# Moving two gate projections out of the opening of an attention, and filling its steps with the output projection

## The chip, the cores and the metric

The kernel runs on one core of a Trainium2 chip. The metric is the device time of one execution in microseconds (us). The kernel before takes 2390.4 us (median of three runs, 2390.4 to 2392.38).

## The reference

A two-layer encoder trunk on 1024 frames of width 1024, all in fp32. Only the mixer of the first layer matters here:

```python
def even_mixer(h, w_in, ..., w_out):
    z = h @ w_in
    uv = gelu(z[..., :1024]); u, v = uv[..., :512], uv[..., 512:]
    q, k, vv, f_logit = the other columns of z      # 8 heads x 64
    y_a = u * (W_s rms_norm(v) + b_s)               # 4 groups x 128 channels
    y_b = forgetting_attention(q, k, vv, log_sigmoid(f_logit))
    return concatenate([y_a, y_b]) @ w_out          # 512 + 512 rows of w_out

def forgetting_attention(...):                      # causal, 8 heads, 8 query blocks of 128
    logits = q.k / 8 + (cumulated log f);  p = softmax(logits);  out = p @ v
```

The residual add, a cross-attention and a feed-forward block follow, and the second layer has another mixer. The change touches none of these.

## The kernel before, in words

**Number format.** Every fp32 operand is split into a high and a low half of a narrower type (fp32r). A product of two operands is three matmuls: high by high, high by low, low by high. All of them are recorded at L539 (`mm`), the low halves at L551 (`low`, on VectorE) or L549 (on GpSimd), the high halves at L557 (`split`, a cast on ScalarE) or, for weights, at L688.

**Order.** The program builds a list of tasks (`self.add`), and `run()` emits them one after the other. A scheduler then arranges the instructions of each engine by data dependence and priority; each engine runs its own list in order. So a task that stands earlier in the list makes its instructions come earlier on several engines at once.

**The gates.** u is computed in four groups of 128 channels. `gate_u(g)` issues 48 matmuls of 128x512 over h, which VectorE reads (L1151) and ScalarE's gelu (L1153) passes on; `gated(g)` is VectorE's product (L1182), which makes y_a of that group.

**The attention.** It runs as a pipeline over 32 steps, 8 heads of 4 query-block pairs (s = 0..31 in the loop). The pipeline opens two steps early (s = -2, -1) with scores alone. Each step has: two score groups on TensorE of widths 128 to 1024 (0.3 to 2 PSUM banks), VectorE's row maximum (L1423), ScalarE's exp (L1425), VectorE's reciprocal (L1429), GpSimd's normalisation (L1430), transposes on TensorE (L1440), cast and low half of the transposed weights (L1443, L551), the product with the values (L539), and a copy and an add (L1474, L1478). exp and gelu need different tables on ScalarE: a change between them is a recorded ACT_TABLE_LOAD.

**The fill.** The half of the output projection that reads y_a does not depend on the attention. It is cut into 32 units (`fill_unit`) of six 128x512 matmuls, which are handed out to the attention's steps. All units share one PSUM bank. After every second unit VectorE adds the bank onto rows of x (L1501), which SP loads from the buffer `xs` in memory (L1494, 512 KB) and stores back (L1505) two units later, one load and one store for four units. The fill needs y_a split into halves: `y_split(g)`, one group a task (L557, L551 of 128x1024).

**Memory.** The split operands live in an arena (`arena_r`). Its first 16K columns, region a, hold h as long as a gate is still to be computed. `close_h` gives them back. Splits of y_a and of the values (`values_in`, L1402) are placed with "ab": in region a where it is free, else in region b.

**The opening of before.** Gates 2 and 3 are tasks of the steps s = -2 and s = -1, behind these steps' scores; h is given back at s = -1, and one y_a group is split in each of the steps s = -2..1. The fill begins at s = 2: two units a step in s = 2..7, one in s = 8..27, none in s = 28..31.

Of the kernel before, what the change touches and what calls it, by code (L numbers as in the profile page):

```python
# [473 lines left out]
class Trunk:  # L474
# [66 lines left out]
    def add(self, fn, ws=(), boost=0):  # L541
        self.tasks.append(Task(fn, ws, boost))
# [331 lines left out]
    def even_in(self):  # L874
# [272 lines left out]
        def gate_u(g, w):  # L1147
            ps = self.B.get(2)
            self.dense(ps, self.h_parts(), self.lhs_from(w, P), KD)
            u = gu[g] = self.F.get(S, "ab")  # L1150
            nc.vector.tensor_tensor(out=u.ap, in0=ps.ap, in1=self.rbc.ap, op=ALU.mult)  # L1151
            ps.free()
            nc.scalar.activation(out=u.ap, in_=u.ap, func=AF.Gelu_apprx_tanh)  # L1153
# [27 lines left out]
        def gated(g):  # L1181
            nc.vector.tensor_tensor(out=self.u[g].ap, in0=self.u[g].ap, in1=gu[g].ap, op=ALU.mult)  # L1182
            gu.pop(g).free()

        wu = [self.w_block(w_in, 0, KD, g * P, P) for g in range(4)]
# [3 lines left out]
        self.add(lambda: (mixed(), gated(0)))  # L1189
        self.add(lambda: (self.fox_open(), gate_u(1, wu[1])), [wu[1]])  # L1190
        self.add(lambda: gated(1))
        self.gates = [[Task(lambda g=g: gate_u(g, wu[g]), [wu[g]]), Task(lambda g=g: gated(g))] for g in (2, 3)]

    def mixing_weights(self):

# [172 lines left out]
    def fox(self):  # L1368
# [39 lines left out]
        def scores(h, p, e):  # L1408
            i = 2 * p + e
            w = (i + 1) * P  # L1410
            qa, ka, qb, kb = (t.ap for t in sets[h % 2])
            ps = self.B.get(1 if w <= 512 else 2, *self.pS)
            q = slice(i * P, (i + 1) * P)
            for c0 in range(0, w, 512):
                n = min(512, w - c0)
                o = ps.ap[:, c0:c0 + n]
                diag = c0 + n == w
                self.mm(o, qa[0:68, q], ka[0:68, c0:c0 + n], True, False)
                self.mm(o, qb[:, q], kb[:, c0:c0 + n], False, not diag)
                if diag:  # L1420
                    self.mm(ps.ap[:, w - P:w], self.identr, self.maskr, False, True)
            m, rs, ri = self.tiny(1), self.tiny(1), self.tiny(1)
            nc.vector.tensor_reduce(out=m, in_=ps.ap[:, 0:w], op=ALU.max, axis=AX.X, negate=True)  # L1423
            pt = self.F.get(w, "ab")
            nc.scalar.activation(out=pt.ap, in_=ps.ap[:, 0:w], func=AF.Exp, bias=m, scale=1.0, accum_out=rs)  # L1425
            ps.free()

            def norm():
                nc.vector.reciprocal(out=ri, in_=rs)  # L1429
                nc.gpsimd.tensor_scalar(out=pt.ap, in0=pt.ap, scalar1=ri, scalar2=1.0, op0=ALU.mult, op1=ALU.mult)  # L1430
            self.defer(norm)
            st["p"][h, i] = pt

        def turn(h, p, c):
            ps = self.B.get(1, *self.pT)
            p0, p1 = st["p"][h, 2 * p], st["p"][h, 2 * p + 1]
            pieces = [(p0, 2 * c), (p1, 2 * c)] + ([(p0, 2 * c + 1)] if c < p else []) + [(p1, 2 * c + 1)]
            n = len(pieces) * P
            for s, (t, j) in enumerate(pieces):
                nc.tensor.transpose(out=ps.ap[:, s * P:(s + 1) * P], in_=t.ap[:, j * P:(j + 1) * P],  # L1440
                                    identity=self.ident)
            th, tl = self.R.get(n, "ab"), self.R.get(n, "ab")
            nc.scalar.copy(out=th.ap, in_=ps.ap[:, 0:n])  # L1443
            st["t"][h, p, c] = th, tl

            def rest():
                self.low(tl.ap, ps.ap[:, 0:n], th.f)
                ps.free()
            self.defer(rest)
            if c == p:  # L1450
                p0.free()
                p1.free()

        def mix(h, p):
            ps = self.B.get(1, *self.pM)
            pr = h // 2
            v = [t.ap.rearrange("p (b e d) -> p b e d", e=2, d=P) for t in st["v"][pr]]
            nj = 2 * p + 2
            for j in range(nj):
                th, tl = st["t"][h, p, j // 2]  # L1460
                lone = j == nj - 1
                c0 = (j % 2) * 256
                n = P if lone else 256
                o = ps.ap[:, 256 - n:256]
                for x, t in enumerate((th, tl)):
                    self.mm(o, v[j // 4][:, j % 4, h % 2, :], t.ap[:, c0:c0 + n], j == 0 and x == 0, lone and x == 1)
            for c in range(p + 1):
                for t in st["t"].pop((h, p, c)):
                    t.free()
            if h % 2 == 0 and p == 0:  # L1470
                self.yb[pr] = self.F.get(S, "b")
            lo = (h % 2) * 64
            tmp = self.F.get(256, "ab")
            nc.scalar.copy(out=tmp.ap[0:64], in_=ps.ap[64:128, 0:256])  # L1474
            yb = self.yb[pr]

            def rest():
                nc.vector.tensor_tensor(out=yb.ap[lo:lo + 64, p * 256:(p + 1) * 256],  # L1478
                                        in0=ps.ap[0:64, 0:256], in1=tmp.ap[0:64], op=ALU.add)
                ps.free()  # L1480
                tmp.free()
                if h == HEADS - 1:
                    self.part_split(3, p * 256, (p + 1) * 256)
            self.defer(rest)

        def y_split(g):
            self.y_a.append(self.split(self.u[g].ap, "ab", S))
            self.u[g].free()
# [26 lines left out]
        add = lambda fn, ws=(): self.add(fn, ws)  # L1515

        def before(h, p):
            if p == 0 and 1 <= h and h + 1 < HEADS:
                heads_in(h + 1)
            if p == 2 and h % 2 == 1 and h + 1 < HEADS:  # L1520
                values_in(h // 2 + 1)
            n = h * 4 + p
            if n == 28:
                for t in sets[0]:
                    t.free()
            if n == 30:
                for t in self.y_a:
                    t[0].free()
                    t[1].free()
                self.open_part(3)  # L1530
            if n in WHOLE:
                self.y_whole(WHOLE.index(n))
# [8 lines left out]
        def close_h():  # L1541
            for b in range(NB):
                self.free_h(b)
            self.rbc.free()
        add(begin)
        wb = [self.w_block(self.a["e_w_out"][0], 512, 4, mp * 256, 256) for mp in range(4)]
        self.wb = wb
        for s in range(-2, len(steps) + 1):
            nxt = steps[s + 2] if s + 2 < len(steps) else None
            cur = steps[s] if 0 <= s < len(steps) else None  # L1550
            old = steps[s - 1] if s >= 1 else None
            turns = [lambda cur=cur, c=c: turn(*cur, c) for c in range(cur[1] + 1)] if cur else []
            if nxt:
                add(lambda nxt=nxt: (scores(*nxt, 0), before(*nxt)))
            if s == len(steps) - 1:
                add(lambda: self.b_part(0, range(0, 3)), [wb[0]])
            if turns:
                add(turns.pop(0))
            if nxt:
                add(lambda nxt=nxt: scores(*nxt, 1))  # L1560
            for t in turns:
                add(t)
            if s == len(steps):
                add(lambda: self.b_part(1, range(0, 3)), [wb[0]])
            if old:
                def fin(old=old):
                    mix(*old)
                    h, p = old
                    if h % 2 == 1 and p == 3:
                        for t in st["v"].pop(h // 2):  # L1570
                            t.free()
                add(fin)
            if s < 0:
                self.tasks.extend(self.gates[s + 2])
            if s == -1:
                add(close_h)
            if s < 2:
                add(lambda g=s + 2: y_split(g))
                continue
            for _ in range(2 if s < 8 else 1):  # L1580
                if fill:
                    self.tasks.append(fill.pop(0))
        assert not fill
# [811 lines left out]
```

## Time and profile before

| | before |
|---|---|
| median of three runs | 2390.4 us |
| the profiled execution's own time | 2389.92 us |
| its span | 2388.1 us |
| mean granted TensorE clock | 0.994 |
| TensorE busy | 2337.4 us (98%) |
| VectorE busy | 1705.6 us (71%) |
| ScalarE busy | 1024.2 us |
| GpSimd busy | 743.0 us |

The shares are means over the whole program. The attention of the first layer lies between about 300 us (its first scores) and 500 us (its last products), and it is read from rows of that stretch. In the rows, PE is TensorE, DVE VectorE, ACT ScalarE, POOL GpSimd, and SPq the issues of SP's DMA queue. Bracketed numbers are idle time before a row's first instruction, with what ended it.

### The profile page before, as it was taken

The page shows a single profiled execution, that of the slowest core. Times are in us where ns is not written, and L with a number is a line of the kernel's source. Part 1 is how long each engine was busy: PE and PEld are TensorE (multiplying, and loading weights), DVE is VectorE, ACT ScalarE, POOL GpSimd, SP SyncE. Part 2 cuts the span into 40 slices and gives each one's busy share as a digit, 9 for nine tenths or more (in the row PEclk, how much of TensorE's full clock was granted, in tenths as well). Part 3 has the DMA queues.
Part 4 walks back from the last instruction along what each step waited for, and adds up shares of the span by engine and source line. Part 5 has one row for each costly group of instructions (what it writes and reads, how often), then busy time and mean ns, then how long its engine had stood idle before and what let it go on. Part 6 is the DMA issues. An engine that isn't in the chain of part 4 may idle for free. (4 is left out here: it accounts for less than half of the span.)

```text
span 2388.1 us, 31149 instructions
## 1 busy us (share of the span) xinstructions
PE 2337.4 (98%) x11358; PEld 1976.5 (83%) x11358; DVE 1705.6 (71%) x2505; ACT 1024.2 (43%) x1866; POOL 743.0 (31%) x745
## 2 busy tenths in 40 slices
PE   7999999999999999999999899999999999999999
PEld 7999879988888878887888788888877887877887
DVE  5456457864898888978677553356879988887666
ACT  6346356755554444445224221146544444444221
POOL 6542333343333343433011310033333334342000
PEclk9999999999999999999999999999999999999999
DMA  7336325431224444438873121021233444357783
GB/s 235 119 133 214 97 81 151 125 124 45 89 70 160 142 149 139 153 131 295 279 267 117 50 65 44 28 79 45 89 101 138 150 141 168 118 194 260 254 289 92
DMA packets 227074, 335.57 MB, mean 141 GB/s; under 512 B 12864, under 2 KB 128664, under 8 KB 226920
## 3 DMA queue, kind: packets, MB, share of 16 engines
q1 hardware_dynamic: 214544, 289.32, 37.1%
q0 software_dynamic: 12192, 44.21, 5.2%
q8 instruction: 89, 1.46, 0.3%
q14 instruction: 65, 0.53, 0.1%
q10 hardware_dynamic: 184, 0.05, 0.0%
HBM read 226.44 MB, written 107.09 MB: 140 GB/s over the span
## 5 line engine op out<-in xcount | busy, mean ns | idle before, releaser
L539 PE MATMUL psum_t<-arena_r 128*128 128x512 f32 (+4 forms) x10304 | 2255.4, 378 | 34.2 <-DVE arena_r L551 10.7
L539 PEld LDWEIGHTS psum_t<-arena_r 128*128 128x128 f32 (+1 forms) x10304 | 1856.2, 189 | 380.1 <-DVE arena_r L551 18.3
L551 DVE TENSOR_TENSOR arena_r<-arena_f,arena_r 128x512 fp32r<-128x512 f32 (+4 forms) x803 | 672.1, 857 | 167.5 <-PE psum_t L539 53.2
L256 ACT CAST arena_r<-arena_f 128x512 fp32r<-128x512 f32 (+2 forms) x504 | 282.4, 584 | 429.4 <-PE psum_t L539 252.6
L2026 POOL TENSOR_TENSOR arena_f<-arena_f 128x512 f32<-128x512 f32 x88 | 164.4, 1874 | 462.4 <-ACT arena_f L2025 462.3
L247 DVE TENSOR_TENSOR arena_f<-arena_f 128x512 f32<-128x512 f32 (+2 forms) x288 | 205.5, 717 | 81.4 <-DMA arena_f<-w_down 48.5
L1973 DVE TENSOR_TENSOR arena_f<-psum_t,arena_f 128x512 f32<-128x512 f32 x208 | 141.7, 685 | 51.6 <-PE psum_t L539 36.0
L2062 ACT CAST arena_r<-arena_f 128x512 fp32r<-128x512 f32 x140 | 86.8, 621 | 160.0 <-DVE arena_f L2033 58.2
L2058 POOL TENSOR_TENSOR arena_f<-arena_f 128x512 f32<-128x512 f32 x80 | 132.0, 1669 | 37.1 <-DVE arena_f L2033 35.6
L2004 DVE TENSOR_TENSOR arena_f<-psum_t,arena_f 128x512 f32<-128x512 f32 x160 | 106.4, 686 | 36.0 <-PE psum_t L539 35.7
L688 ACT CAST arena_r<-arena_f 128x1024 fp32r<-128x1024 f32 (+1 forms) x57 | 59.0, 1042 | 128.9 <-PE psum_t L539 90.3
L803 POOL TENSOR_TENSOR arena_f<-arena_f 128x1024 f32<-128x1024 f32 x21 | 60.6, 2884 | 127.8 <-ACT arena_f L802 61.9
L551 DVE TENSOR_TENSOR arena_r<-psum_t,arena_r 128x512 fp32r<-128x512 f32 (+3 forms) x124 | 84.6, 703 | 18.7 <-ACT arena_r L1443 6.8
L2025 ACT ACTIVATE arena_f<-arena_f 128x512 f32<-128x512 f32 x88 | 55.6, 632 | 81.6 <-DVE arena_f L2024 81.6
L236 POOL DMA_DIRECT2D arena_f<-w_down x38 | 30.3, 799 | 191.7 <-DVE arena_r L551 107.1
L1430 POOL TENSOR_SCALAR arena_f<-arena_f,small 128x640 f32<-128x640 f32 (+6 forms) x64 | 49.5, 781 | 108.8 <-DVE small L1429 104.7
L2033 DVE TENSOR_TENSOR arena_f<-arena_f 128x512 f32<-128x512 f32 x88 | 76.4, 868 | 4.5 <-POOL arena_f L2026 0.5
L2024 DVE TENSOR_TENSOR arena_f<-arena_f 128x512 f32<-128x512 f32 x88 | 66.2, 752 | 1.1 <-ACT arena_f L831 1.1
L562 POOL TENSOR_TENSOR small<-small,mhalf 128x4 f32<-128x4 f32 (+1 forms) x64 | 63.7, 995 | 5.2
L1425 ACT ACTIVATE arena_f<-psum_t,small 128x640 f32<-128x640 f32 (+6 forms) x64 | 47.5, 745 | 23.1 <-DVE small L1423 20.2
L2261 POOL TENSOR_TENSOR arena_f<-arena_f 128x1024 f32<-128x1024 f32 x4 | 10.4, 2598 | 139.5 <-DVE arena_f L2213 139.5
L1753 POOL TENSOR_SCALAR arena_f<-arena_f,small 128x256 f32<-128x256 f32 x64 | 33.3, 538 | 65.2 <-DVE small L1750 50.8
(192 smaller groups left out, 1533.9 us busy)
## 6 DMA issues: line engine op xcount, KB each, us to landing
pq<-arena_r SPq DMA_DIRECT2D x140, 512.0 KB
arena_r<-pq SPq DMA_DIRECT2D x280, 256.0 KB
arena_f<-w_gate SPq DMA_DIRECT2D x22, 1024.0 KB
arena_f<-w_up SPq DMA_DIRECT2D x22, 1024.0 KB
arena_r<-qk SPq DMA_DIRECT2D x48, 256.0 KB
qk<-arena_r POOLq DMA_DIRECT2D x16, 512.0 KB, 4.1
arena_f<-xa_wkv SPq DMA_DIRECT2D x16, 512.0 KB
arena_f<-xs SPq DMA_DIRECT2D x16, 512.0 KB
```

The source lines that it names most:

```text
L247: getattr(T.nc, self.adds).tensor_tensor(out=out, in0=a, in1=b, op=what)
L256: T.nc.scalar.copy(out=hv, in_=src)
L539: self.nc.tensor.matmul(out=out, lhsT=lhsT, rhs=rhs, start=start, stop=stop, skip_group_check=again)
L551: getattr(self.nc, eng).tensor_tensor(out=out, in0=src, in1=high, op=ALU.subtract)
L562: self.nc.gpsimd.tensor_tensor(out=out, in0=in_, in1=self.mhalf[:, 0:in_.shape[-1]], op=ALU.pow)
L1973: nc.vector.tensor_tensor(out=o, in0=bank[q].ap, in1=o if other is None else other, op=ALU.add)
L2004: nc.vector.tensor_tensor(out=o, in0=bank[q].ap, in1=o, op=ALU.add)
L2024: nc.vector.tensor_tensor(out=q, in0=q, in1=r, op=ALU.mult)
L2026: nc.gpsimd.tensor_tensor(out=q, in0=q, in1=r, op=ALU.mult)
L2033: nc.vector.tensor_tensor(out=c[j].ap[:, o], in0=c[j].ap[:, o], in1=s.ap[:, o], op=ALU.mult)
L2058: nc.gpsimd.tensor_tensor(out=out, in0=a, in1=b, op=ALU.subtract)
L2062: nc.scalar.copy(out=t.ap[:, 0:512], in_=src)
```

## The change

Gates 2 and 3 become ordinary tasks right behind gate 1, before the attention is opened. h is given back before the attention opens, so the values of the first two heads and all four y_a splits are placed where h was. Two y_a groups are split in s = -2 and two in s = -1. The fill begins at s = -1: two units a step in s = -1..5, one in s = 6..23, none in s = 24..31.

```diff
@@ even_in
         self.add(lambda: gated(1))
-        self.gates = [[Task(lambda g=g: gate_u(g, wu[g]), [wu[g]]), Task(lambda g=g: gated(g))] for g in (2, 3)]
+        for g in (2, 3):
+            self.add(lambda g=g: gate_u(g, wu[g]), [wu[g]])
+            self.add(lambda g=g: gated(g))
@@ fox
+        add(close_h)
         add(begin)
@@ fox, at the end of each step s
             if s < 0:
-                self.tasks.extend(self.gates[s + 2])
-            if s == -1:
-                add(close_h)
-            if s < 2:
-                add(lambda g=s + 2: y_split(g))
-                continue
-            for _ in range(2 if s < 8 else 1):
+                add(lambda g=2 * s + 4: y_split(g))
+                add(lambda g=2 * s + 5: y_split(g))
+            for _ in range(0 if s < -1 else 2 if s < 6 else 1):
                 if fill:
                     self.tasks.append(fill.pop(0))
```

The two added lines move every line behind them down by two, so L1425 of before is L1427 of after, and L1501 is L1503.

TensorE before, from the last 47 matmuls of gate 2 to the scores of 640 behind gate 3 (the last 48 matmuls of 128x512 in two rows; 128x128 on maskr is the causal mask of a score group):

```order
L539 MATMUL psum_t<-arena_r 128x512 x47
L539 MATMUL psum_t<-arena_r 128x384 [waits DVE_49]
L539 MATMUL psum_t<-arena_r 128x384
L539 MATMUL psum_t<-maskr,identr 128x128
L539 MATMUL psum_t<-arena_r 128x512 x2
L539 MATMUL psum_t<-maskr,identr 128x128
L539 MATMUL psum_t<-arena_r 128x512 [waits DVE_49]
L539 MATMUL psum_t<-arena_r 128x512 x47
L539 MATMUL psum_t<-arena_r 128x512 [waits Activation_49]
L539 MATMUL psum_t<-arena_r 128x512
L539 MATMUL psum_t<-arena_r 128x128 [waits Activation_49]
L539 MATMUL psum_t<-arena_r 128x128
```

Here a score group of 384 and one of 512 stand between the gates 2 and 3, and the scores of 640 come behind gate 3. TensorE after, behind gate 3, from the scores of 512 to the first fill unit (the three matmuls that wait for DVE and Activation, for DVE, and for Pool, are its first) and the first scores of 768:

```order
L539 MATMUL psum_t<-arena_r 128x512 x2
L539 MATMUL psum_t<-maskr,identr 128x128
L539 MATMUL psum_t<-arena_r 128x512 [waits DVE_49]
L539 MATMUL psum_t<-arena_r 128x512
L539 MATMUL psum_t<-arena_r 128x128 x2
L539 MATMUL psum_t<-maskr,identr 128x128
L539 MATMUL psum_t<-arena_r 128x512 [waits DVE_49,Activation_49]
L539 MATMUL psum_t<-arena_r 128x512 [waits DVE_49]
L539 MATMUL psum_t<-arena_r 128x512 [waits Pool_49]
L539 MATMUL psum_t<-arena_r 128x512 [waits Activation_49] x2
L539 MATMUL psum_t<-arena_r 128x512
L539 MATMUL psum_t<-arena_r 128x512 [waits DVE_49]
```

Gates 1 to 3 now stand one behind the other, 144 matmuls, with five score groups (128 to 640) behind them and the first fill unit next. Of the row x2 that waits for Activation the first is the unit's fourth matmul, which waits for the cast of y_a's group 1; the second begins the scores of 768, which take the PSUM columns of the scores of 128 and wait for their exp. The rest of the fill unit stands behind them.

ScalarE before, around gate 3's end (L1153 is a gelu, L1443 the cast of transposed weights):

```order
L557 CAST arena_r<-arena_f 128x1024 [waits PE_49] x2
L688 CAST arena_r<-arena_f 128x1024 [waits DMAHW5_49,PE_49]
L1443 CAST arena_r<-psum_t 128x384 [waits PE_49]
L1153 ACT_TABLE_LOAD
L1153 ACTIVATE arena_f<-arena_f 128x1024 [waits DVE_49]
L1425 ACT_TABLE_LOAD [waits DVE_49]
L1425 ACTIVATE arena_f,small<-psum_t,small 128x768 [waits Activation_49]
L1474 COPY arena_f<-psum_t 64x256 [waits DVE_49,PE_49]
L1425 ACTIVATE arena_f,small<-psum_t,small 128x896 [waits DVE_49]
L1425 ACTIVATE arena_f,small<-psum_t,small 128x640 [waits DVE_49]
L557 CAST arena_r<-arena_f 128x1024
L1443 CAST arena_r<-psum_t 128x512 [waits PE_49]
```

and after, from the values' casts (L1404) on:

```order
L1404 CAST arena_r<-arena_f 128x8x64 [waits PE_49] x2
L557 CAST arena_r<-arena_f 128x1024 [waits Activation_49]
L557 CAST arena_r<-arena_f 128x1024
L557 CAST arena_r<-arena_f 128x1024 [waits DVE_49]
L688 CAST arena_r<-arena_f 128x1024 [waits DMAHW5_49,PE_49,Activation_49]
L1153 ACTIVATE arena_f<-arena_f 128x1024 [waits DVE_49]
L1427 ACT_TABLE_LOAD [waits DVE_49]
L1427 ACTIVATE arena_f,small<-psum_t,small 128x128 [waits Pool_49]
L1427 ACTIVATE arena_f,small<-psum_t,small 128x256 [waits DVE_49]
L1427 ACTIVATE arena_f,small<-psum_t,small 128x384 [waits DVE_49,Pool_49]
L1427 ACTIVATE arena_f,small<-psum_t,small 128x640 [waits DVE_49,PE_49]
L1427 ACTIVATE arena_f,small<-psum_t,small 128x512 [waits DVE_49]
```

The exps of 128 to 512 stood ahead of gate 3's end and stand behind it now, and behind the casts of y_a's groups 0 to 2, a weight's cast and the gelu of gate 3; the table is changed once in this stretch.

SP's queue before, the first two loads of x rows and the first store (qk and cs are the loads for head 2):

```order
L1494 DMA arena_f<-xs 128x1024 [waits DMAHW5_49,DMASW7_49,DMAHW7_49,Activation_49,Pool_49]
L1387 DMA arena_r<-qk 64x1024 [waits DMAHW0_49,DMASW0_49,PE_49]
L1388 DMA arena_r<-qk 64x1024 [waits DMAHW1_49,DMASW7_49,DMASW1_49]
L1389 DMA arena_r<-cs 2x1024 [waits DMAHW2_49]
L1390 DMA arena_r<-cs 2x1024 [waits DMAHW3_49]
L1391 DMA arena_r<-qk 64x1024 [waits DMAHW4_49,PE_49]
L1392 DMA arena_r<-qk 64x1024
L1393 DMA arena_r<-qk 64x1024 [waits DMAHW6_49]
L1394 DMA arena_r<-qk 64x1024 [waits DMAHW7_49]
L1494 DMA arena_f<-xs 128x1024 [waits DMAHW0_49,DVE_49]
L697 DMA arena_f<-e_w_out 128x4x256 [waits DMAHW1_49,PE_49,Pool_49]
L1505 DMA xs<-arena_f 128x1024 [waits DMAHW2_49,DMAHW0_49,DVE_49]
```

and after:

```order
L1496 DMA arena_f<-xs 128x1024 [waits DMAHW1_49,DMASW7_49,DVE_49]
L1389 DMA arena_r<-qk 64x1024 [waits DMAHW2_49,DMASW0_49,PE_49]
L1390 DMA arena_r<-qk 64x1024 [waits DMAHW3_49,DMASW7_49]
L1391 DMA arena_r<-cs 2x1024 [waits DMAHW4_49]
L1392 DMA arena_r<-cs 2x1024 [waits DMAHW5_49]
L1393 DMA arena_r<-qk 64x1024 [waits DMAHW6_49,PE_49]
L1394 DMA arena_r<-qk 64x1024 [waits DMAHW7_49]
L1395 DMA arena_r<-qk 64x1024 [waits DMAHW0_49]
L1396 DMA arena_r<-qk 64x1024 [waits DMAHW1_49]
L1507 DMA xs<-arena_f 128x1024 [waits DMAHW2_49,DVE_49]
L1496 DMA arena_f<-xs 128x1024 [waits PE_49,DMAHW3_49,Activation_49,Pool_49]
L1496 DMA arena_f<-xs 128x1024 [waits DMAHW4_49,DMAHW2_49]
```

Before, the second load (the last L1494) goes out ahead of the first store (L1505) into a second buffer. After, the third load shown (the last L1496, rows of the second four units) goes into the buffer of the first, and stands behind the store (L1507) that empties it. The L1496 ahead of it loads the rows of the third four units.

## Rows read from the trace of the kernel before

**Rows 1.** The page: span and busy time of TensorE.
```profile
span 2388.1 us, 31149 instructions
...
PE 2337.4 (98%) x11358; PEld 1976.5 (83%) x11358; DVE 1705.6 (71%) x2505; ACT 1024.2 (43%) x1866; POOL 743.0 (31%) x745
```

**Rows 2.** Timeline of TensorE, opening: start us, busy us, instructions [idle before].
```profile
312.22 11.75 PE L539 MATMUL psum_t<-arena_r 128*128 128x512 f32 x52
...
328.14 2.01 PE L539 MATMUL psum_t<-arena_r 128*128 128x512 f32 x9 [1.03 <-DVE arena_r L551]
331.37 1.20 PE L539 MATMUL psum_t<-arena_r 68*128 68x512 f32 x4 [1.22 <-ACT arena_f L1425]
...
332.89 0.54 PE L539 MATMUL psum_t<-arena_r 68*128 68x128 f32 x2 [0.26 <-ACT arena_f L1425]
...
336.95 1.42 PE L1440 MATMUL psum_t<-ident,arena_f 128*128 128x128 f32 x11 [0.53 <-POOL arena_f L1430]
...
344.24 2.11 PE L539 MATMUL psum_t<-arena_r 128*128 128x512 f32 x8 [0.94 <-DVE arena_f L1501]
```

**Rows 3.** Windows of 2 us: length, busy by engine, PEclk, DMA share, GB/s.
```profile
332.00:334.00 2.00, 1.74 (x9) 1.44 (x8) 1.50 (x4) 2.00 (x5) 0.63 (x1) 0.80 0.09 35
334.00:336.00 2.00, 2.00 (x11) 1.91 (x9) 1.68 (x4) 1.16 (x3) 1.95 (x2) 0.50 1.00 252
336.00:338.00 2.00, 1.47 (x11) 1.06 (x11) 1.32 (x5) 2.00 (x6) 1.52 (x2) 0.84 1.11 225
```

**Rows 4.** Timeline of ScalarE, opening.
```profile
304.19 0.37 ACT L1425 ACTIVATE arena_f<-psum_t,small 128x128 f32<-128x128 f32 x1
...
322.68 2.00 ACT L557 CAST arena_r<-arena_f 128x1024 fp32r<-128x1024 f32 x2 [6.31 <-PE psum_t L539]
324.59 1.04 ACT L688 CAST arena_r<-arena_f 128x1024 fp32r<-128x1024 f32 x1
...
326.02 1.28 ACT L1153 ACT_TABLE_LOAD   x1
...
329.03 1.28 ACT L1425 ACT_TABLE_LOAD   x1 [0.66 <-DVE small L1423]
330.33 0.90 ACT L1425 ACTIVATE arena_f<-psum_t,small 128x768 f32<-128x768 f32 x1
```

**Rows 5.** Timeline of VectorE, opening.
```profile
301.70 0.61 DVE L1423 TENSOR_REDUCE small<-psum_t 128x1 f32<-128x128 f32 x2
...
323.36 1.23 DVE L1151 TENSOR_TENSOR arena_f<-psum_t,arena_f 128x1024 f32<-128x1024 f32 x1 [6.80 <-PE psum_t L539]
324.50 1.22 DVE L551 TENSOR_TENSOR arena_r<-arena_f,arena_r 128x1024 fp32r<-128x1024 f32 x1
...
343.50 0.69 DVE L1501 TENSOR_TENSOR arena_f<-psum_t,arena_f 128x512 f32<-128x512 f32 x1 [2.20 <-DMA arena_f<-xs]
```

**Rows 6.** Timeline of SP's queue: two loads of x rows.
```profile
336.82 0.54 SPq L1494 DMA_DIRECT2D arena_f<-xs  x1
...
453.10 0.35 SPq L1494 DMA_DIRECT2D arena_f<-xs  x1
```

**Rows 7.** Timeline of VectorE, first add of the last unit's rows.
```profile
456.42 0.69 DVE L1501 TENSOR_TENSOR arena_f<-psum_t,arena_f 128x512 f32<-128x512 f32 x1 [0.15 <-DMA arena_f<-xs]
```

**Rows 8.** Timeline of TensorE, end of the attention.
```profile
479.26 1.20 PE L539 MATMUL psum_t<-arena_r 68*128 68x512 f32 x4 [0.84 <-ACT arena_f L1425]
...
485.43 0.33 PE L1440 MATMUL psum_t<-ident,arena_f 128*128 128x128 f32 x1 [1.62 <-POOL arena_f L1430]
...
487.33 1.47 PE L1440 MATMUL psum_t<-ident,arena_f 128*128 128x128 f32 x12
488.56 11.63 PE L539 MATMUL psum_t<-arena_r 128*128 128x256 f32 x61
```

**Rows 9.** Windows of 10 us, columns as in rows 3.
```profile
460.00:470.00 10.00, 10.00 (x66) 8.97 (x65) 9.74 (x22) 7.34 (x18) 4.12 (x6) 1.00 0.44 147
...
480.00:490.00 10.00, 8.38 (x61) 7.53 (x61) 8.53 (x16) 8.46 (x16) 4.02 (x3) 1.00 0.50 168
```

## The prediction

> **What bounds the kernel now.** I read the page first: TensorE is busy for 2337.4 of 2388.1 us [rows 1]. The change adds and removes no matmul, so what it can win or lose is TensorE's idle time in the stretch it touches, and a low clock there. The timeline of TensorE's opening comes next. Behind gate 3, a row of 11.75 us that runs without a gap, it stops five times up to the first add of the fill, for 0.26 to 1.22 us, 3.98 us together [rows 2]. The gaps end with VectorE's low halves, ScalarE's exps, GpSimd's normalisation and the first add onto x rows: the pipeline is starting and there is no fill yet. Third, windows of 2 us: the granted clock there is 0.80, 0.50 and 0.84, so half speed (1.2 instead of 2.4 GHz) for part of 6 us, after TensorE had stopped; 0.4 + 1.0 + 0.32 = 1.7 us [rows 3]. Last, the end of the attention, with no fill: gaps of 0.84 and 1.62, 2.46 us [rows 8], while VectorE is busy 8.53 of 10 us [rows 9]. So the stretch holds 3.98 + 1.7 + 2.46 = 8.1 us that an order of the same work could win.
>
> **The gates, moved (TensorE 0; what is hidden).** 96 matmuls of 128x512 at 11.75 / 52 = 0.226 us [rows 2] go ahead of the scores of 384 and 512, which now follow. The same columns run, so 0 by itself. But the gates were also cover: while gates 2 and 3 ran for 23 us, ScalarE did the exps of 128 to 512 and waited 6.31 us afterwards [rows 4]. Now those exps stand behind gate 3's end. That is the price that I look for in the opening.
>
> **The opening, hand chain, t = 0 at gate 3's end.** The values' casts and y_a's casts go where h was, so they wait for gate 3's last reads. ScalarE in its new order: the values done at 0.5 (they start a little before the end, estimate from half of a 1.04 cast), three y_a casts at 1.0 each, 3.5; the weight's cast 1.04, 4.55; the gelu of as many columns taken alike, 5.6; table 1.28, 6.9; exp of 128, 0.37, 7.25 [rows 4]. VectorE: the read of gate 3, 1.23, ends at 1.4; row maxima of 128, 256 and 384, 1.1, to 2.5; low half of y_a's group 0, 1.22, to 3.7 [rows 5]. TensorE: five score groups to 1.9, and one fill matmul that needs the cast alone, 2.1. The second needs the low half: idle to 3.7, 1.6. Three matmuls to 4.4. Next in its queue are the scores of 768, whose PSUM columns are freed by the exp of 128: idle to 7.25, 2.85, and behind them is queued the rest of the fill unit, though its operands are there by 6.2 (two maxima and a second low half behind 3.7). Later the fourth y_a cast (1.04) stands on ScalarE ahead of the exp of 768: about 0.75 more. Sum 5.2, against 3.98 before: **+1.2**. Bounds: below, all five gaps of before vanish, -4.0. Above, TensorE has nothing more than scores, one fill unit and the scores of 768 (1.9 + 1.4 + 0.6) until the exp of 768 ends. That is at 11.7, with four exps of 0.37 to 0.90 (about 2.5), the fourth cast and the 0.90 behind 7.25 [rows 4]: idle 7.8, +3.8. I take the chain's own value. The first add's 2.20 us of waiting for x rows [rows 5] needs no term: that load now goes out ahead of the loads for head 2.
>
> A table load counts only where ScalarE ends a gap. Of before's loads two lie behind gate 3 (326.02 and 329.03), one remains there; the 1.28 saved is in the chain above [rows 4]. The next exp starts 1.30 after the load's start, so nothing but the load shows [rows 4].
>
> **The clock: 0.** Before's clock fell after gaps of 1.03 and 1.22 us [rows 2, 3]. The new gaps are longer, and TensorE's clock may fall for as long or longer; I take the same 1.7, with no fall and twice the fall as bounds, -1.7 to +1.7.
>
> **The splits and the fill, moved up.** 32 units of six matmuls run as before, one per step less crowded. What changes is which steps go without.
>
> *x rows: +0.7.* Rows of the second four units are loaded into the buffer of the first, behind its store, and the third add on VectorE waits for that load, with the pipeline's maxima and low halves queued behind it and TensorE behind those. A load of these rows alone takes 453.10 to 456.42, 3.3 us; one with eight other loads ahead of it 336.82 to 343.5, 6.7 us [rows 5 to 7]. The second add comes at about 17.5 on my chain; a store (taken as a load, 3.3 and up to 6.7, since no row shows its end) and a load follow, so the data come 6.6 to 10 later, while the third add would be ready 6 to 7 later. VectorE waits 0 to 4, and TensorE has the matmuls of about 3 us ahead of it: 0 to 2.5. I take 0.7, nearer to 3.3 because the eight loads are through by then.
>
> The Trainium skill ("DMA: Bandwidth & Descriptors", section "Anatomy of one DMA — SWDGE (gpsimd) path") puts about 2.0 us of fixed cost on each DMA, most of it the receipt of the write, heaviest for HBM, and speaks so against a store with a load behind it: it is paid twice. By its figures 512 KB takes an estimated 2.0 + 1.2 = 3.2 us, with which the trace's 3.3 agrees, and the pair 6.4; no run here shows the store, and by the page the term would be 0.
>
> *The end: +1.5.* Four more steps, one head, have no fill: four units of 6 x 0.226 = 1.36, 5.4 us that TensorE has had there as cover and now has earlier. Without it a head's 36 transposes, at (488.56 - 487.33) / 12 = 0.1 each [rows 8], and the 19,456 columns of its scores and value products, at 0.226 for 512, take TensorE 3.7 + 8.6 = 12.3 us. With the fill that is 17.7, of which VectorE is busy for 9.74 of 10 [rows 9]: 17.2, and 15.8 without the two adds of 0.69 [rows 7]. So a head without fill is longer on VectorE than on TensorE. Bounds: 0, because the head is off the end and the waits overlap, and +5.4, where the end is VectorE's. Between them before's own stretch without fill: 2.46 idle over about 61 transposes behind the last unit, so 1.45 for 36.
>
> *Everything else: 0*, within 2 either way, an estimate (half of the opening's 3.98): the scheduler also shifts loads and weight splits in other places, and TensorE gets no new wait there.
>
> **Sum.** 1.2 + 0 + 0.7 + 1.5 + 0 = +3.4. The profiled execution took 2389.92, 0.48 below the median of 2390.4; 2389.92 + 3.4 = 2393.3 by that execution, **2393.8** by the median. A difference of 0.2%, 4.8 us, is about what a measurement of this kernel can tell from no change. So the forecast is a small loss within that.
>
> **Rivals.**
> 1. *Faster.* The fill does what a fill does: the five gaps of the opening close and the clock is not lowered, -4.0 - 1.7 = -5.7, while the end keeps its 2.46. 2384.7; with the end's +1.5, 2386.2. For it: four of the five gaps end with engines that had no other TensorE work beside them [rows 2]. Against it: in the new order the first fill stands behind splits that cannot start before h is free, and then behind a bank that waits for ScalarE. Chance 0.14.
>    The Trainium skill ("ScalarE: Activation LUTs", section "What ACT_TABLE_LOAD costs") gives 1.28 for the load and 1.38 more for a drain, 2.66 a switch; by that the one switch fewer behind gate 3 gives 1.4 more than the chain has and the opening would be -0.2 instead of +1.2. The trace disagrees on the drain: the exp begins 0.02 after the load [rows 4].
> 2. *Slower than 0.2%.* The end becomes VectorE's: from the point at which the fill is used up, each of TensorE's 12 us a head waits for VectorE, and the 5.4 of fill is simply missing: +5.4 instead of +1.5. For it: VectorE at 9.74 [rows 9] with fill in the windows, and gaps as soon as the fill ends [rows 8]. Against it: 8.53 without fill, so VectorE is not full there. With the opening's +1.2 and the x rows' +0.7 this is +7.3, 2397.7; with the x rows at 2.5 and the clock at +1.7, +10.8, 2401.2. Chance 0.34.
> 3. *Nothing happens.* The gaps are only moved: the idle time of a starting pipeline is the same wherever the fill stands, and the end's new gaps are inside before's. 0 to +1, 2390.4 to 2391.4. For it: equal work and TensorE at 98%. Chance 0.2.
> The forecast itself, +1.5 to +4.8, has 0.32.
>
> **Range and chances.** Forecast and rival 3 give "same" 0.52, rival 1 "faster" 0.14, rival 2 "slower" 0.34. Range 2385.5 to 2401: from rival 1 with the end's loss to rival 2 with its second price. The forecast's own range is 2391.5 to 2396.
>
> **What would show each step.** In TensorE's timeline behind gate 3: gaps before the second fill matmul (low half) and before the scores of 768 (exp, L1427), about 1.6 and 2.9; if they are not there, the first rival holds. Window clocks below 1.00 in the 10 us behind. On VectorE: a wait of the third add (L1503) for x rows. At the end: gaps behind the last fill that add up to about 4 instead of 2.5; 7 or more would be the second rival. The forecast is wrong if TensorE's idle time between 290 and 490 us differs from before's by less than 1 or more than 6 us, or if it changes elsewhere.

## The result, and the profile after

The changed kernel takes 2403.2 us (median of six runs, 2400.81 to 2405.12), before in the same comparison 2390.23: ratio 1.005, 95% interval 1.0039 to 1.006. It is slower, by 13 us where 3.4 were forecast, and outside the range. The page of the profiled execution (2405.12 us) shows 5 us more of TensorE's busy time and 10 us more of its idle time than [rows 1]:

```profile
span 2403.3 us, 31133 instructions
...
PE 2342.6 (97%) x11358; PEld 1977.1 (82%) x11358; DVE 1711.3 (71%) x2505; ACT 1019.1 (42%) x1862; POOL 737.2 (31%) x745
```

Two landmarks cut the program: VectorE's first L1165 (a gate group's result, ahead of everything that moves) and its last add of the attention, L1478 before and L1480 after. Start us, busy us, of before and then after:

```profile
280.77 1.28 DVE L1165 SCALAR_TENSOR_TENSOR arena_f<-psum_t,gc,arena_f 128x1024 f32<-128x1024 f32 x1 [1.41 <-PE psum_t L539]
...
497.38 0.42 DVE L1478 TENSOR_TENSOR arena_f<-psum_t,arena_f 64x256 f32<-64x256 f32 x1 [3.46 <-ACT arena_f L1474]
```

```profile
280.97 1.28 DVE L1165 SCALAR_TENSOR_TENSOR arena_f<-psum_t,gc,arena_f 128x1024 f32<-128x1024 f32 x1 [1.40 <-PE psum_t L539]
...
508.54 0.42 DVE L1480 TENSOR_TENSOR arena_f<-psum_t,arena_f 64x256 f32<-64x256 f32 x1 [5.01 <-ACT arena_f L1476]
```

Between them lie 216.61 us before and 227.57 after: the attention loses 11.0. From there to VectorE's last instruction of the program, a copy, it is 4.0 more. TensorE's gaps after, to be read against [rows 2] and [rows 8]:

```profile
325.46 0.96 PE L539 MATMUL psum_t<-arena_r 128*128 128x512 f32 x3 [0.97 <-DVE arena_r L551]
328.79 1.77 PE L539 MATMUL psum_t<-arena_r 68*128 68x512 f32 x7 [2.37 <-ACT arena_f L1427]
...
424.57 3.26 PE L539 MATMUL psum_t<-arena_r 128*128 128x512 f32 x14 [1.56 <-DVE arena_f L1503]
436.80 1.20 PE L1442 MATMUL psum_t<-ident,arena_f 128*128 128x128 f32 x9 [0.48 <-ACT arena_f L1427]
...
473.17 0.92 PE L539 MATMUL psum_t<-arena_r 128*128 128x512 f32 x2 [1.55 <-DVE arena_r L551]
...
493.58 0.33 PE L1442 MATMUL psum_t<-ident,arena_f 128*128 128x128 f32 x1 [3.25 <-DVE arena_r L551]
...
548.91 3.72 PE L539 MATMUL psum_t<-arena_r 128*128 128x512 f32 x15 [1.51 <-ACT arena_r L790]
```

The opening has two gaps of 3.34 us instead of five of 3.98. What is new lies later: behind an add onto x rows at 424, twice at the end, and once behind the attention. Behind each gap of the end the granted clock falls to half for a while (windows of 2 us, columns as in [rows 3]):

```profile
330.00:332.00 2.00, 2.00 (x8) 1.53 (x7) 2.00 (x6) 0.70 (x3) 0.03 (x1) 0.55 0.00 0
332.00:334.00 2.00, 2.00 (x11) 1.52 (x9) 1.18 (x4) 2.00 (x4) 2.00 (x4) 0.60 0.00 0
...
474.00:476.00 2.00, 2.00 (x12) 2.00 (x10) 1.79 (x8) 1.99 (x7) 1.19 (x2) 0.50 0.77 232
476.00:478.00 2.00, 2.00 (x15) 1.81 (x13) 1.15 (x3) 0.13 (x2) 1.29 (x3) 0.76 0.11 30
...
494.00:496.00 2.00, 2.00 (x12) 2.00 (x11) 0.75 (x4) 0.37 (x1) 1.12 (x1) 0.51 0.04 10
496.00:498.00 2.00, 2.00 (x14) 2.00 (x13) 0.74 (x2) 0.40 (x1) 0.00 (x0) 0.64 0.00 0
```

That is 1.7 us in the opening, as before, and 1.7 twice at the end (with 0.89 at 472), which before had not. Up to the last add, gaps of 10.7 instead of 6.4 and clock of 5.1 instead of 1.7 make 7.7 of the 11.0 (two gaps of 0.25 and 0.30 are not shown). Another 1.6 is no loss but work that moved: between the landmarks TensorE runs seven more matmuls of 128x512 (436 for 429, at 0.226 us), output matmuls that now stand ahead of the last add. What the other 1.7 are wasn't settled.

### The profile page after: what moved, and what is told of

Read it like the earlier page. It is cut to its first block, busy times and chain, and to the rows that moved or that the text cites. A ratio compares the mean times of both kernels' runs of the same rounds, so it can differ in the third digit from the quotient of the medians.

```text
span 2403.3 us, 31133 instructions
## 1 busy us (share of the span) xinstructions
PE 2342.6 (97%) x11358; PEld 1977.1 (82%) x11358; DVE 1711.3 (71%) x2505; ACT 1019.1 (42%) x1862; POOL 737.2 (31%) x745
## 5 line engine op out<-in xcount | busy, mean ns | idle before, releaser
L539 PE MATMUL psum_t<-arena_r 128*128 128x512 f32 (+5 forms) x10304 | 2259.6, 379 | 42.3 <-DVE arena_r L551 17.3
L1432 POOL TENSOR_SCALAR arena_f<-arena_f,small 128x896 f32<-128x896 f32 (+6 forms) x64 | 48.3, 763 | 103.5 <-DVE small L1431 102.1
L1427 ACT ACTIVATE arena_f<-psum_t,small 128x896 f32<-128x896 f32 (+6 forms) x64 | 47.6, 747 | 23.5 <-DVE small L1425 13.4
L2260 POOL TENSOR_TENSOR arena_f<-arena_f 128x1024 f32<-128x1024 f32 x4 | 10.4, 2601 | 139.5 <-DVE arena_f L2212 139.5
L1425 DVE TENSOR_REDUCE small<-psum_t 128x1 f32<-128x640 f32 (+5 forms) x64 | 47.2, 750 | 8.2 <-PE psum_t L539 7.7
```

Of the source, the lines that this page charges most:

```text
L539: self.nc.tensor.matmul(out=out, lhsT=lhsT, rhs=rhs, start=start, stop=stop, skip_group_check=again)
```

## The experiments

"Attention" is the time between the two landmarks less before's 216.61; "behind" is the change of the time from the last add to VectorE's last copy of the program (L2344 in before). Both are of one profiled execution, which need not be a typical one: e12's took 2384.67 us, 7.2 less than its median. Medians and ratios are of the timed runs, each against before in its own comparison.

| run | median | ratio, interval | attention | behind |
|---|---|---|---|---|
| changed kernel | 2403.2 | 1.005, 1.0039 to 1.006 | +11.0 | +4.0 |
| e1 fill to step 27 | 2411.27 | 1.0098, 1.0084 to 1.0112 | +8.5 | +12.0 |
| e2 before, fill to 23 | 2397.42 | 1.004, 1.0026 to 1.0054 | +1.3 | +5.9 |
| e3 gates only | 2409.95 | 1.0091, 1.0078 to 1.0105 | +5.1 | +9.9 |
| e4 fill to 30 | 2415.42 | 1.0117, 1.0098 to 1.0136 | +17.1 | +11.4 |
| n1 before, shifted | 2401.4 | 1.005, 1.0038 to 1.0063 | +0.4 | +9.9 |
| n2 after, shifted | 2410.64 | 1.0085, 1.0069 to 1.0102 | +8.8 | +9.2 |
| e6 rows ahead | 2406.44 | 1.007, 1.0056 to 1.0084 | +5.0 | +10.4 |
| e7 part later | 2403.17 | 1.0053, 1.0039 to 1.0068 | +11.9 | +1.0 |
| s before, end f | 2388.75 | 1.0002, 0.9993 to 1.0012 | -0.1 | -2.5 |
| s after, end f | 2403.16 | 1.0066, 1.0051 to 1.0081 | +9.7 | +7.1 |
| s before, end r | 2386.12 | 0.9994, 0.9984 to 1.0003 | +0.1 | -4.1 |
| s after, end r | 2401.7 | 1.0058, 1.0043 to 1.0073 | +10.8 | +0.9 |
| e10 gates alone | 2399.5 | 1.0041, 1.0028 to 1.0055 | -2.2 | +14.0 |
| e9 gates only, b | 2395.37 | 1.003, 1.0019 to 1.0042 | -4.0 | +10.6 |
| e8 after, region b | 2390.83 | 1.0011, 1.0002 to 1.002 | +1.1 | +0.1 |
| n3 before, shifted | 2387.57 | 0.9995, 0.9986 to 1.0004 | -0.1 | -1.7 |
| e11 e9, end r | 2397.76 | 1.0041, 1.0028 to 1.0055 | -4.0 | +12.8 |
| e12 e9, end f | 2391.91 | 1.0013, 1.0005 to 1.0022 | -4.2 | +0.4 |

**The fill's schedule.** e1 and e3 are the changed kernel, e2 is before, each with one line edited:

```diff
e1  -for _ in range(0 if s < -1 else 2 if s < 6 else 1):
    +for _ in range(0 if s < -1 else 2 if s < 2 else 1):
e2  -for _ in range(2 if s < 8 else 1):
    +for _ in range(2 if s < 12 else 1):
e3  +for _ in range(0 if s < 2 else 2 if s < 8 else 1):
e4  +for _ in range(0 if s < -1 else 1):   # y_a freed in end()
```

> The changed kernel with the same 32 fill units spread differently: two in each of the steps -1 to 1, then one a step to step 27, as late as in the kernel before. Theory A (the steps 24 to 31 without fill cost the end: gaps of 1.55 and 3.25 us and 3.4 us of clock instead of 2.46 us and none): the gaps and the low clock at the end go back to those of before, the attention's end comes 5 to 7 us earlier than in the changed kernel, total 2394 to 2398. Theory B (the moved gates cost it, by lost cover in the opening): nothing changes, 2401 to 2405. Theory C (the scheduler's reshuffled order in the rest of the program is the loss): total anywhere within 2397 to 2405, with the attention's end moving by less than 2 us.

> The kernel before with its gates and splits where they were; only the fill is pulled forward: two units a step in steps 2 to 11, one in 12 to 23, none in 24 to 31. Theory A: the end loses its cover alone, TensorE's idle time behind the last unit rises from 2.46 us to 5 to 7 us and the clock falls there, total 2395 to 2399. Theory B or C: within 2 us of before, 2388 to 2392.

> The changed kernel (gates 2 and 3 ahead, h given back, y_a split in two steps) with the fill in the steps of the kernel before (two a step in 2 to 7, one in 8 to 27). Theory A: the end is like before's; the opening has neither gates nor fill as cover and its idle time rises from 3.5 us to 6 to 10 us; total 2393 to 2398. Theory B: the whole loss stays, 2401 to 2405. If the opening needs no cover at all: 2390 to 2392.

> The changed kernel with one fill unit in every step from -1 to 30; the halves of y_a are kept to the end of the attention instead of being freed at step 28. Theory A: the end is covered better than in the kernel before (its 2.46 us of gaps shrink below 1.5), and the opening has half of the changed kernel's fill: total 2387 to 2391. Theory B: 2400 to 2404. Theory C: anywhere, with the end's gaps unrelated to the fill.

Theory A, that the loss is the end without fill, falls. e1's fill lasts as long as before's, and its end still has a gap of 3.24 us with the clock down behind it; e2's longest is 1.17 with the clock up, and its attention loses 1.3. (e2's total lies in theory A's range, but by 5.9 us behind the attention; those of e1, e3 and e4 lie above every range that was named.) e3's attention loses 5.1 with the fill as before, 4.4 of it between its last two adds. Nine matmuls of the attention's own output half, which in before stand behind the last scores, stand ahead of them, and nothing is left for the wait behind them. They are the first nine of the row of 17, which merges shapes; its last four are those scores.

```profile
479.49 3.75 PE L539 MATMUL psum_t<-arena_r 128*128 128x512 f32 x17 [0.27 <-DVE arena_r L551]
...
487.81 0.33 PE L1442 MATMUL psum_t<-ident,arena_f 128*128 128x128 f32 x1 [3.21 <-DVE arena_r L551]
```

e3's gaps are no longer in sum than before's (6.6 for 6.4); 3.4 of the loss is clock, half of it in the opening, and 2.0 is nine more matmuls of 128x512 ahead of the last add.

e4 waits for x rows six times on VectorE, 0.99 to 3.41 us each. And e1 and e3 lose 10 to 12 us behind the attention, where no task was edited: theory C had something, too.

**Layout by itself.** The arenas hand out the block that has been free longest, so one block more shifts all later ones, and with them the order. n1 and n2 take and free 64 columns of the fp32 arena in `begin`, n3 of the split one; the four s runs do it in `end`, behind the attention.

```diff
+            self.F.get(64, "b").free()     # n3 and "r": self.R.get
```

> The kernel before with one 64-column block of the fp32 arena taken and given back at the attention's opening. No instruction is added or removed; only which free block the later tasks get, and by that the order in which the scheduler lays out the rest of the program. Theory C (a new placement and order by itself moves the time by several us): total differs from before by 3 us or more, in either direction, and the difference arises after the attention too. Theory A or B (what the change says is what costs): within 2 us of before.

> The changed kernel with the same block taken and given back at the same place. Theory C: total differs from the changed kernel's 2403 by 3 us or more, and may come near before's. Theory A or B: within 2 us of 2403.

> The kernel before with one 64-column block of the fp32 arena taken and given back when the attention is over, so that only the placement and order of what follows differ. Theory C (the kernel before stands on a layout of the later phases that most others don't reach): the attention's last add stays within 2 us of before's, the total rises by 4 to 14 us, 2394 to 2403. Rival (layouts scatter evenly round before's): anywhere within 6 us either way, as often below as above.

> The changed kernel with the same block at the same place. If the attention alone carries the change's own effect, its last add stays 9 to 11 us behind before's counted from the opening's start, and the total is 7 to 13 us above that of the kernel before with the same block. Rival (the loss is all layout): the two are within 4 us of each other.

> As the first of this call, with the block taken from the arena of split operands instead. Theory C: total 2394 to 2403, attention as before. Rival: within 6 us either way.

> The changed kernel with that block. Own effect in the attention: 7 to 13 us above the kernel before with the same block. All layout: within 4 us of it.

> The kernel before with one 64-column block of the arena of split operands taken and given back at the attention's opening; no instruction differs. If layouts scatter widely (n1), 3 us or more from before; if n1 was a rare one, within 2 us. The attention itself stays within 2 us in both.

n1 alone gives +12 us with no task changed, nearly all of it behind the attention; the other three shifts of before give -2 to +1. So layout scatters, but before's time is no rare one. With the same shift in both, the changed kernel is slower by 9.2 (n), 14.4 (f) and 15.6 (r), and its attention by 8.3, 9.8 and 10.7: the loss in the attention is the change's own. Two of the three totals are above the 7 to 13 that were expected.

**Two waits of the changed kernel, taken away.** e6 loads the next x rows at the second unit of the four before; e7 moves the first output part of the last step behind its transposes.

```diff
e6  +            if half == 0 and part == 1 and m + 1 < KD:
    +                st["nx"] = load(m + 1)
    # e6's load() and the use of st["nx"] are left out here
e7  -            if s == len(steps) - 1:                 # ahead of the turns
    -                add(lambda: self.b_part(0, range(0, 3)), [wb[0]])
    +            if s == len(steps) - 1:                 # behind them
    +                add(lambda: self.b_part(0, range(0, 3)), [wb[0]])
```

> The changed kernel with each load of x rows issued three fill units earlier (at the second unit of the four before). Theory: the waits of VectorE's adds for x rows (2.82 us at 424 us, with 1.56 us of TensorE behind it) go; the attention ends 1.5 to 2.5 us earlier, 2400 to 2402. Rival: another wait takes their place, or the placement of the second buffer moves the rest of the program by more than that.

> The changed kernel with the 18 matmuls of the first output unit of the attention's own half (b_part 0) put behind the last step's transposes instead of ahead of them. Theory: the gap of 3.25 us at 493.6 us arises because these matmuls are used up 5 us before it, while the weight casts and the low halves stand ahead of the last transposed weights on ScalarE and VectorE; put behind, they fill it: the gap falls below 1 us, the clock there stays up, the attention's last add comes 3 to 5 us earlier, total 2398 to 2401. Rival: the scheduler places them by readiness anyway, gap and time stay, 2402 to 2405.

In e6 no add waits for x rows, and the attention is 5.9 shorter where 1.5 to 2.5 were expected; 10.4 behind it eat that. More than the wait went: the gaps at the end are 2.7 us for the changed kernel's 4.8, the longest 0.78, and the clock stays up there. In e7 the gap at the end stays, 3.06 us, now ended by GpSimd's normalisation, and so does the time, as its rival had it. The nine output matmuls did move, but behind the transposes that wait (to 499.00 and later), so they fill nothing.

**The homes.** e10 moves the gates and nothing else. e9 is e3, and e8 the changed kernel, with two homes put back:

```diff
-            v = [self.R.get(1024, "ab") for _ in range(2)]
+            v = [self.R.get(1024, "ba" if pr == 0 else "ab") for _ in range(2)]
-            self.y_a.append(self.split(self.u[g].ap, "ab", S))
+            self.y_a.append(self.split(self.u[g].ap, "ba" if g == 0 else "ab", S))
```

> The kernel before with gates 2 and 3 moved ahead and nothing else: h is released at step -1, y_a is split in steps -2 to 1 and the fill runs in steps 2 to 27, as before. Theory D (the early release of h and the new homes cost the end): the attention's last add is within 1.5 us of before's from the opening's start, the last step's gap is below 2 us, total 2389 to 2394. Theory E (the gates as such cost it): the last add 4 to 6 us late as in the run with the gates moved and h released early, gap of about 3.2 us, total 2395 or more.

> The run with gates moved, h released early and the fill as before (e3), with the values of the first two heads and y_a's group 0 placed in region b as in the kernel before, so that they don't wait for gate 3's last reads. Theory D: the end's gap falls from 3.2 to below 2 us and the last add comes 3 to 5 us earlier than e3's. Theory E: the end stays; only the opening's first gap (1.1 us, VectorE's low half) goes.

> The changed kernel with the same two homes. The opening: the first fill unit doesn't wait for the low half of group 0 any more, its gap of 0.97 us goes, the one before the scores of 768 (2.37 us, exp) shrinks by the two casts that leave ScalarE's queue behind gate 3, to about 0.5 to 1.5. Theory D: the end's 3.25 goes as well, total 2394 to 2398. Theory E: it stays, 2400 to 2403.

Theory D holds in the attention. e10's is 2.2 shorter than before's, so the gates cost nothing there; its total misses theory D's range, since 14.0 are lost behind. From e3 to e9 the two homes give 9.0 us, from the changed kernel to e8 9.8, and by medians e8 is 3.0 above before where the changed kernel is 13.0. Of the two gains 2.2 and 3.8 are gaps and 3.4 and 5.1 clock; the rest is matmuls of 128x512 that no longer run ahead of the last add (15 and 7). e8's gaps, opening and end:

```profile
326.75 0.98 PE L539 MATMUL psum_t<-arena_r 68*128 68x512 f32 x4 [1.18 <-ACT arena_f L1427]
...
329.61 0.33 PE L1442 MATMUL psum_t<-ident,arena_f 128*128 128x128 f32 x1 [0.64 <-POOL arena_f L1432]
...
466.94 0.44 PE L539 MATMUL psum_t<-arena_r 68*128 68x128 f32 x2 [0.99 <-ACT arena_f L1427]
...
470.05 0.39 PE L539 MATMUL psum_t<-arena_r 128*128 128x256 f32 x1 [0.51 <-ACT arena_r L1445]
...
481.59 2.33 PE L539 MATMUL psum_t<-arena_r 128*128 128x512 f32 x9
...
486.19 1.31 PE L539 MATMUL psum_t<-arena_r 128*128 128x256 f32 x9 [1.17 <-ACT arena_f L1427]
```

The wait for the low half is gone from the opening, since group 0 and the values no longer wait for gate 3; that is 3.0 us, 1.3 of gaps and 1.7 of clock, which doesn't fall. Most of the rest is the end: nine output matmuls stand behind the last scores again, and on VectorE a row maximum stands between the two low halves of 128x1024 that in the changed kernel ran for 2.81 us in one piece ahead of the transposed weights. VectorE of the changed kernel, then of e8:

```profile
471.44 2.81 DVE L551 TENSOR_TENSOR arena_r<-arena_f,arena_r 128x1024 fp32r<-128x1024 f32 x2
```

```profile
465.74 1.21 DVE L551 TENSOR_TENSOR arena_r<-arena_f,arena_r 128x1024 fp32r<-128x1024 f32 x1
466.88 0.54 DVE L1425 TENSOR_REDUCE small<-psum_t 128x1 f32<-128x384 f32 x1
467.34 1.21 DVE L551 TENSOR_TENSOR arena_r<-arena_f,arena_r 128x1024 fp32r<-128x1024 f32 x1
```

That the homes change this order 140 us later is shown; by which chain of blocks and priorities isn't. Nor are the new homes enough for the bad order. e6 has them, and there, too, row maxima stand between the two low halves and nine output matmuls (485.33) behind the last scores:

```profile
469.72 1.20 DVE L551 TENSOR_TENSOR arena_r<-arena_f,arena_r 128x1024 fp32r<-128x1024 f32 x1
470.85 0.74 DVE L1425 TENSOR_REDUCE small<-psum_t 128x1 f32<-128x384 f32 x2
471.51 1.36 DVE L551 TENSOR_TENSOR arena_r<-arena_f,arena_r 128x1024 fp32r<-128x1024 f32 x1
```

So putting the homes back is one way out of that order, and loading the rows earlier is another.

**e9 with another layout behind it.**

> e9 (gates ahead, fill as before, first values and first y_a group in region b) with one 64-column block of the arena of split operands taken and given back when the attention is over. If e9's loss behind the attention is layout alone: the attention's last add stays 3 to 5 us ahead of before's, and the total moves away from e9's 2395 by 3 us or more in either direction; with the layout luck of before it would be 2384 to 2386. If the loss follows from the attention's new form: total stays 2393 to 2397.

> The same with the block of the fp32 arena. Layout alone: the total differs from the run before in this call and from e9 by 3 us or more, the attention's last add again 3 to 5 us ahead of before's. New form: 2393 to 2397.

The attention stays 4 us ahead in both; behind it 12.8 and 0.4 are lost. TensorE is idle there for 36.9 and 31.2 us, in e9 for 36.7 and in before for 30.9: one of the two layouts takes that idle time away, the other doesn't. But the 0.4 is of e12's fastest execution. By medians e9, e11 and e12 are 7.5, 10.6 and 4.7 us above before. So layout moves e9's loss by some us; that it is layout alone isn't shown. No version was faster than before.

## Why the prediction was wrong

- *The gates and the opening (+1.2).* Right in mechanism, wrong in sign. The two gaps are where it put them, 0.97 and 2.37 for 1.6 and 2.85: the scores and the first fill matmul ran to 324.49, 2.7 us behind the start of VectorE's read of gate 3 (321.81, at 0.2 on the chain) for 2.1 worked out, the exp of 128 ended 6.8 us behind it for 7.25, and the third gap (0.75) didn't come. The two add up to 3.34 for 5.2, and against before's 3.98 this is -0.6. The drain that the Trainium skill ("ScalarE: Activation LUTs", section "What ACT_TABLE_LOAD costs") puts behind a table load isn't seen here either; ScalarE of the changed kernel:

```profile
326.99 1.28 ACT L1427 ACT_TABLE_LOAD   x1
328.28 0.37 ACT L1427 ACTIVATE arena_f<-psum_t,small 128x128 f32<-128x128 f32 x1
```

- *The clock (0).* Right for the opening of this execution, and luck: n2 and e7, with the same two gaps to 0.01 us, lost 3.4 there, which is the upper bound. It was not asked for at the end, where two falls cost 3.4.
- *The x rows (+0.7).* The third add waited 1.15 us for its load, and TensorE not at all: the store went out at 342.16 and the add began at 349.41, 7.3 us for the pair of store and load where 6.6 to 10 were allowed. The wait came at the 13th add (423.83, 2.82 us; load issued at 417.61, behind eight loads and a weight), with 1.56 us of TensorE: the mechanism, at another place and twice the size. The 6.4 that the prediction works out for the pair comes from a section on DMAs that GpSimd issues; the pair here is SP's. SP's queue, then VectorE, of the changed kernel:

```profile
342.16 0.35 SPq L1507 DMA_DIRECT2D xs<-arena_f  x1
...
417.61 0.35 SPq L1496 DMA_DIRECT2D arena_f<-xs  x1
```

```profile
349.41 0.69 DVE L1503 TENSOR_TENSOR arena_f<-psum_t,arena_f 128x512 f32<-128x512 f32 x1 [1.15 <-DMA arena_f<-xs]
...
423.83 0.69 DVE L1503 TENSOR_TENSOR arena_f<-psum_t,arena_f 128x512 f32<-128x512 f32 x1 [2.82 <-DMA arena_f<-xs]
```

- *The end (+1.5).* **The step that failed.** It took the missing fill as the only cost and put the clock there at nothing without a reason. Fill pulled forward alone costs 1.3 (e2, near the 1.5), but in the changed kernel the end has 4.8 us of gaps for 2.46 and 3.4 of clock, +5.7. The gaps alone are near the "about 4" of its sign; the clock is the larger part. What brought this about is an order that came with the new homes of the values and of y_a, which the prediction named ("go where h was") and priced in the opening only. With the homes of before the change's attention loses 1.1 (e8). The chain from homes to order stays open, and e6 leaves that order with the new homes in place. The fill isn't free of guilt: with the gates ahead, early fill costs 5.1 (e9 to e8) and 5.9 (e3 to the changed kernel). So the 11.0 add up from runs as -4.0 (gates and early splits with the homes of before, e9), +5.1 (early fill, e8) and +9.8 (the homes).
- *Everything else (0, within 2).* The bound was far too narrow: behind the attention the runs lie between -4.1 and +14.0, and the changed kernel at +4.0, where a gap of 1.51 (548.91) is new. By its last sign, too, the forecast was wrong: the idle time changes outside 290 to 490 us, at 493.58 and 548.91. The second rival had the size (+7.3 to +10.8) and the place, but not the cause, and its sign, gaps of 7 us or more at the end, didn't show.

## What to carry to other kernels

When a scheduler and rotating buffers lay out the program, an edit that only moves tasks also moves homes, and a home changes waits and orders far from the edit: ask of each moved task where its outputs now live and whose last read they wait for, and put the homes back as a test. Time a few versions of both kernels with a shifted layout before a difference of half a per cent is put down to an edit. Count a fall of the clock, 1.7 us here, as possible with every new gap and not only where it fell before: here one followed a gap of 1.55 us. And when an instruction of one engine serves as a landmark, count the other engines' work in front of it: seven matmuls had moved across this one.

## What the hardware showed

The clock's fall isn't a fixed price of a gap. In n2 TensorE waits 3.25 us as in the changed kernel, and the windows behind stay at 1.00, where the changed kernel's showed 0.51 and 0.64:

```profile
491.28 0.33 PE L1442 MATMUL psum_t<-ident,arena_f 128*128 128x128 f32 x1 [3.25 <-DVE arena_r L551]
```

```profile
492.00:494.00 2.00, 2.00 (x20) 2.00 (x19) 0.82 (x4) 0.78 (x2) 1.12 (x1) 1.00 0.03 8
494.00:496.00 2.00, 2.00 (x17) 1.87 (x17) 1.58 (x4) 1.77 (x5) 0.00 (x0) 1.00 0.00 0
```

So a difference of 1.7 us between two profiled executions can be one such fall.
